# Key norms of an RWKV-7 mixer from compact tiles with tokens on the partitions, and gate and merge matmuls dealt in half steps to the recurrence's chunks

## Chip, cores and metric

One core of one Trainium2 chip. The metric is the device time of one execution in microseconds (us): the median of three runs.

## What is computed

The reference is a two-layer encoder trunk on 512 tokens of width 1024, in float32. Each layer has a mixer with three branches (pooling, differential attention, a bidirectional RWKV-7 recurrence), merged by sigmoid gates, then an output projection, a layer norm, a squared-ReLU MLP and another layer norm. The parts that the change touches:

```python
kk = kh * heads(k_k)                                   # 8 heads of 64
kk = kk / max(sqrt(sum(kk * kk, -1, keepdims=True)), 1e-12)
y  = wkv7_scan(..., kk, a, forward) + wkv7_scan(..., kk, a, reverse)
...
branch = einsum('bsnc,ncd->bsnd', [y_a, y_b, y_c], w_branch)
gates  = sigmoid(gl + b_gate)                          # 3 x 1024 columns of x @ w_in
mixer  = sum(gates * branch, over the 3 branches) @ w_out
```

## The kernel before

Activations lie transposed: channels on the 128 partitions, the 512 tokens on the free axis. Almost every product of a dense weight is taken three times in a 32-bit replicated form (`mm3`: high x high, high x low, low x high), so each weight tile is split into a high part (a ScalarE cast, L142) and a low part (a subtraction, L143, mostly on GpSimd). A dense tile of 128 output channels is 8 x 3 = 24 matmuls of 512 columns.

A layer runs in stages, in `layer`:

1. `rw_prep` makes the recurrence's factors, channel tile by channel tile (j = 0 to 3); `weave` deals pooling and attention matmuls between its steps. A generator yields the microseconds of TensorE work that it has emitted, and `weave` hands out filler until its sum is `ratio` times the main generator's sum.
2. `rw_solve`, first part: a triangular solve, thirty dependent pairs of VectorE operations (L650, L652). The filler is `gates(0)` and `merge(0)`; what is left of it is drained.
3. `rw_solve`, second part: small matmuls (32 or 64 rows and columns) that build the matrix `tt`. Six steps of `merge(1)` are emitted first, and the rest is dealt at ratio 0.8. These filler steps are emitted by `behind`: on TensorE they may not go ahead of the last small matmul before them.
4. `rw_chain`: eight chunks of 64 tokens, c = 0 to 7, each with steps that depend on each other: `pb x suv`, the products of the next chunk's rows, `x tt`, `qk` and `rq`, and two groups of transposed copies. Here TensorE's order is the order in which the code emits (a manual schedule); on the other engines and on the DMA queues the planner of the framework chooses the order from a simulated timeline. Each chunk loads the next one's products `ch` by DMA; `ch` has two buffers, and its load can begin only when the last group of transposes of the chunk has read the old one.
5. The end of the chain: from chunk 6 the filler is `rw_out(0)` (group norm and gate of the middle tokens) and what is left of the gates. Then `rw_out(1)` (the outer tokens) with the first four steps of `merge_last`, and the rest of `merge_last`, the projection and the MLP.

For the key norms, `rw_prep` squares a key tile, `head_sums` sums the squares per head with two 512-column matmuls against a block of ones (L528, L529), which leaves each head's sum on all its 64 partitions, and `rsqrt` takes the inverse root of the 128 x 512 tile by a bit shift and three Newton steps on VectorE (L211 to L218).

Of the kernel before, what the change touches and what calls it, by code (L numbers as in the profile page):

```python
# [18 lines left out]
S = 512  # L19
# [30 lines left out]
FILL = (1.7, 25.0, 2.0, 1.2, 1.2, 6, 0.8)  # L50
# [71 lines left out]
class Enc:  # L122
# [81 lines left out]

    def rsqrt(self, pool, x, shape, tags, bufs=1, out=None):

        V = self.nc.vector
        t = self.T(pool, shape, tags[0], bufs)
        g = t.bitcast(I32)
        y = self.T(pool, shape, tags[1], bufs, I32)  # L210
        V.tensor_scalar(g, x.bitcast(I32), 1, None, ALU.logical_shift_right)  # L211
        V.tensor_scalar(y, g, -1.0, float(0x5F3759DF), ALU.mult, ALU.add)
        yf = y.bitcast(F32)
        out = yf if out is None else out
        for i in range(3):
            V.tensor_tensor(t, yf, yf, ALU.mult)
            V.scalar_tensor_tensor(t, t, -0.5, x, ALU.mult, ALU.mult)
            V.scalar_tensor_tensor(out if i == 2 else yf, t, 1.5, yf, ALU.add, ALU.mult)  # L218
        return out
# [160 lines left out]
    def layer(self, l):  # L380
# [6 lines left out]
        with tc.tile_pool(name=f"R{l}", bufs=1) as self.R:  # L387
            rt = ExitStack()
            with ExitStack() as at:
                self.AT = at.enter_context(tc.tile_pool(name=f"AT{l}", bufs=1, side="right"))  # L390
                self.RX = at.enter_context(tc.tile_pool(name=f"X{l}", bufs=1, side="right"))
                att = chain(self.pool_branch(), self.attention())
                with tc.tile_pool(name=f"A{l}", bufs=1) as self.R1:
                    weave(self.rw_prep(), att, FILL[0], FILL[1])
                    drain(att)
                self.RT = rt.enter_context(tc.tile_pool(name=f"T{l}", bufs=1))
                with tc.tile_pool(name=f"B{l}", bufs=1) as self.R2:
                    fill = chain(self.gates(0), self.pool_load(), self.merge(0))
                    steps = self.rw_solve()
                    weave(self.urgent(steps), fill, FILL[2])  # L400
                    drain(fill)
                    fill = chain(self.merge(1), self.gates(2))
                    for _ in range(int(FILL[5])):
                        next(fill)
                    fill = self.behind(fill)
                    weave(self.urgent(steps), fill, FILL[6])
            with rt, tc.tile_pool(name=f"C{l}", bufs=1) as self.R3:
                steps = self.rw_chain()
                with tc.manual_schedule(engines={mybir.EngineType.PE}):
                    weave(self.urgent(steps), fill, FILL[3])  # L410
                    fill = alternate(self.rw_out(0), fill)
                    weave(self.urgent(steps), fill, FILL[4])
                    drain(fill)
                last = self.merge_last()
                weave(self.urgent(self.rw_out(1)), self.behind(islice(last, 4)), 1.0)
# [53 lines left out]
    def rw_prep(self):  # L469
# [5 lines left out]
        pss = self.lora_ps  # L475
        if l == 0:
# [15 lines left out]
        for j in range(4):  # L492
# [3 lines left out]
            ps = self.head_sums(sq)  # L496
            rs = self.T(R1, [128, S], "sq", 1)
            V.tensor_scalar(rs, ps, 1e-24, None, ALU.max)
            rs = self.rsqrt(R1, rs, [128, S], ("ld", "ta"))
            kk = self.T(R1, [128, S], "kk", 1)  # L500
            V.scalar_tensor_tensor(kk, k, self.pcol(P_KK + j), rs, ALU.mult, ALU.mult)
# [17 lines left out]
            yield 0.4  # L519

# [580 lines left out]
    def gate(self, n, m, gw, dst):  # L1101
# [3 lines left out]
        for k in range(NK):  # L1105
            self.mm3(ps, wh[:, k, :], wl[:, k, :], self.xh[:, k, :], self.xl[:, k, :], k == 0, k == NK - 1)
            if k % 4 == 3:
                yield 2.6
# [21 lines left out]
    def merge(self, n):  # L1130
# [5 lines left out]
        for m in range(NK):  # L1136
# [8 lines left out]
            for k in range(4):  # L1145
                self.mm3(ps, wh[:, k], wl[:, k], *y[k], k == 0, k == 3)
            V.scalar_tensor_tensor(g, g, 1.0, ps, ALU.add, ALU.mult)
            if n:
                nc.gpsimd.tensor_tensor(self.mg[m], self.mg[m], g, ALU.add)
            yield 2.6  # L1150
# [190 lines left out]
```

## Time and profile before

| | |
|---|---|
| median of three runs | 2178.73 us (2174.46 to 2180.32) |
| the profiled execution | 2177.25 us, span 2175.4 us |
| TensorE (PE) busy | 2070.0 us, 95% of the span |
| VectorE (DVE) busy | 1109.1 us, 51% |
| ScalarE (ACT) busy | 858.7 us, 39% |
| GpSimd (POOL) busy | 611.5 us, 28% |
| mean granted TensorE clock | 0.961 of full speed |

Matmuls overlap each other in the pipeline, so a busy TensorE is not one at its peak; a matmul's row gives its length from start to end, and the distance between the starts of neighbours is what it costs. The clock has two levels, 1.2 GHz (0.50) and 2.4 GHz (1.00); a figure between them is a mean over a stretch. 2177.25 us is the profiled execution's own time, 1.85 us more than its span.

### The profile page before, as it was taken

The numbers are of one execution on the slowest core, as the hardware profiler recorded it, in microseconds if no ns is written. First come the engines' busy times: TensorE is split into PE (matmuls) and PEld (weight loads), VectorE is DVE, ScalarE is ACT, GpSimd is POOL, SyncE is SP. The second block draws the span as 40 slices with busy tenths as digits, with TensorE's granted clock in tenths as the row PEclk, the third lists the DMA queues.
The fourth block names the chain that finished last, engine by engine and source line by source line (L and its number), as shares of the span: only waits on it lengthen the run. The fifth ranks groups of instructions, "written<-read, shape, count | busy, mean of one in ns | idle before, by whom it ended". The sixth has DMA issues, their size and how long they took to land.

```text
span 2175.4 us, 32525 instructions
## 1 busy us (share of the span) xinstructions
PE 2070.0 (95%) x13382; PEld 1647.2 (76%) x13382; DVE 1109.1 (51%) x1760; ACT 858.7 (39%) x1341; POOL 611.5 (28%) x407
## 2 busy tenths in 40 slices
PE   6999999999979999999998999999998899999998
PEld 5667776777767888888886776778777688888886
DVE  5878769322246443343266878782222445423423
ACT  5355555324323332232344555562333243322322
POOL 4543353133215400000445433431322163000004
PEclk9999999889979999999999999997999799999999
DMA  6343341145523332332424334411545052323322
GB/s 209 115 131 105 121 156 59 40 110 148 137 72 119 98 93 97 97 97 97 140 93 131 120 97 128 134 59 38 151 130 148 21 176 67 97 97 97 90 95 87
DMA packets 309680, 233.63 MB, mean 107 GB/s; under 512 B 50106, under 2 KB 277880, under 8 KB 309532
## 3 DMA queue, kind: packets, MB, share of 16 engines
q1 hardware_dynamic: 309388, 231.30, 35.6%
q8 instruction: 105, 1.72, 0.3%
q10 hardware_dynamic: 144, 0.26, 0.1%
q14 instruction: 43, 0.35, 0.1%
HBM read 200.05 MB, written 31.47 MB: 106 GB/s over the span
## 4 chain that ended last, share of the span: by engine, by line
PE 67%; DVE 14%; DMA 7%; POOL 4%; ACT 4%; issue 3%; SPq 0%; POOLq 0%; DVEq 0%; ACTq 0%
PE d L166 13%; PE d L168 12%; PE d L167 12%; PE a L162 5%; PE c L162 3%; DMA ch<-sc 3%; PE l L166 2%; PE l L167 2%; PE l L168 2%; DVE x L652 2%; PE t L162 2%; DVE at L650 1%; PE a L166 1%; PE a L167 1%; PE a L168 1%
## 5 line engine op out<-in xcount | busy, mean ns | idle before, releaser
L166 PE MATMUL d<-xh,wh 128*128 128x512 f32 (+1 forms) x1360 | 546.8, 402 | 6.7 <-ACT xh L268 2.4
L168 PE MATMUL d<-xh,wl 128*128 128x512 f32 (+1 forms) x1360 | 538.8, 396 | 0.8 <-POOL wl L143 0.7
L167 PE MATMUL d<-xl,wh 128*128 128x512 f32 (+1 forms) x1360 | 537.4, 395 | 0.0
L143 POOL TENSOR_TENSOR wl<-wraw,wh 128x1024 fp32r<-128x1024 f32 x137 | 337.9, 2468 | 530.1 <-ACT wh L142 507.1
L142 ACT CAST wh<-wraw 128x1024 fp32r<-128x1024 f32 x259 | 271.3, 1048 | 517.8 <-PE d L167 208.0
L143 DVE TENSOR_TENSOR wl<-wraw,wh 128x1024 fp32r<-128x1024 f32 x122 | 160.6, 1317 | 368.2 <-ACT wh L142 368.1
L166 PEld LDWEIGHTS d<-xh,wh 128*128 128x128 f32 x1360 | 258.9, 191 | 78.9 <-issue 14.1
L168 PEld LDWEIGHTS d<-xh,wl 128*128 128x128 f32 x1360 | 258.8, 190 | 67.0 <-issue 7.1
L167 PEld LDWEIGHTS d<-xl,wh 128*128 128x128 f32 x1360 | 259.3, 191 | 57.6 <-issue 3.1
L143 POOL TENSOR_TENSOR wrl<-wraw,wrh 128x1024 fp32r<-128x1024 f32 x16 | 39.2, 2465 | 659.6 <-ACT wrh L142 659.6
L1266 ACT CAST hh<-f 128x512 fp32r<-128x512 f32 x64 | 39.7, 622 | 84.5 <-DVE f L1263 84.5
L1267 DVE TENSOR_TENSOR hl<-f,hh 128x512 fp32r<-128x512 f32 x64 | 44.2, 693 | 41.4 <-ACT hh L1266 41.3
L795 DVE COPY x<-c 128x256 f32<-128x256 f32 x16 | 6.8, 424 | 112.7 <-ACT x L794 112.7
L977 ACT ACTIVATE p<-p,mx 128x512 f32<-128x512 f32 x64 | 46.0, 719 | 43.6 <-DVE mx L976 43.3
L162 PE MATMUL a<-ch 64*128 64x128 f32 x512 | 53.0, 311 | 10.6 <-DMA ch<-sc 10.6
L162 PEld LDWEIGHTS a<-ch 64*128 64x128 f32 x512 | 42.5, 206 | 15.1 <-issue 7.0
L652 DVE TENSOR_TENSOR x<-x,at 128x60 f32<-128x60 f32 (+14 forms) x60 | 51.1, 851 | 1.5
L1263 DVE TENSOR_TENSOR f<-f 128x512 f32<-128x512 f32 x64 | 43.6, 684 | 14.8 <-ACT f L1262 14.8
L758 DVE TENSOR_TENSOR rq<-a,cst 128x256 f32<-128x256 f32 x64 | 27.2, 425 | 44.1 <-PE a L162 31.6
L975 DVE CUSTOM_DVE_ANT_0 p<-l,tb 128x512 f32<-128x512 f32 x64 | 42.5, 683 | 13.8 <-PE t L990 9.6
L168 PE MATMUL l<-wh,hl 128*128 128x512 f32 x112 | 43.6, 389 | 0.0
L167 PE MATMUL d<-wl,hh 128*128 128x512 f32 x112 | 43.6, 389 | 0.0
(531 smaller groups left out, 4039.3 us busy)
## 6 DMA issues: line engine op xcount, KB each, us to landing
wraw<-in_w_in_dram SPq DMA_DIRECT2D x110, 512.0 KB
wraw<-in_w_up_dram SPq DMA_DIRECT2D x64, 512.0 KB
wraw<-in_w_down_dram SPq DMA_DIRECT2D x64, 512.0 KB
sc<-st SPq DMA_DIRECT2D x16, 1280.0 KB
ch<-sc SPq DMA_DIRECT2D x32, 640.0 KB
wraw<-in_w_branch_dram SPq DMA_DIRECT2D x24, 512.0 KB
wraw<-in_w_out_dram SPq DMA_DIRECT2D x16, 512.0 KB
xs<-s SPq DMA_DIRECT2D x16, 256.0 KB
```

Source lines behind the costliest of these rows:

```text
L142: self.nc.scalar.copy(hi, src)
L143: (eng or self.nc.vector).tensor_tensor(lo, src, hi, ALU.subtract)
L162: self.anchor = self.nc.tensor.matmul(*args, **kw).ins
L166: mm(out, wh, xh, start=first, stop=False)
L167: mm(out, wh, xl, start=False, stop=False)
L168: mm(out, wl, xh, start=False, stop=last)
L652: V.tensor_tensor(ab[:, s + 1:, :, :s], ab[:, s + 1:, :, :s], w, ALU.add)
L975: V.tensor_tensor_reduce(p, ps, bias, op0=ALU.add, op1=ALU.max, scale=1.0, scalar=-3e38, accum_out=mx)
L977: A.activation(p, p, AF.Exp, bias=mx, accum_out=sm[:, m:m + 1])
L1263: V.tensor_tensor(f, f, f, ALU.mult)
L1266: A.copy(hi, f)
L1267: V.tensor_tensor(lo, f, hi, ALU.subtract)
```

## The change

It has two parts. First, the key norms: the sums per head are taken with the tokens on the partitions (four matmuls with the squares as the stationary operand and two columns of ones moving), which gives a 128 x 8 tile; VectorE clamps it, GpSimd raises it to the power -0.5, TensorE transposes it, ScalarE and VectorE split it into a high and a low part, and eight 128-column selector matmuls spread it over the heads' partitions in PSUM, where `kk`'s multiplication reads it. `rsqrt` goes.

Second, the filler: `gate` and `merge` yield after 6 matmuls (1.3) instead of 12 (2.6); the six steps ahead of the second part of the solve go; the chain's ratio is 0.7 instead of 1.2 up to chunk 5 and 1.4 instead of 1.2 after it; the end deals `rw_out(0)` and then `rw_out(1)` in turn with whatever filler is left, all in the manual order.

```diff
-FILL = (1.7, 25.0, 2.0, 1.2, 1.2, 6, 0.8)
+FILL = (1.7, 25.0, 2.0, 0.7, 1.4, 0.8)
...
                     fill = chain(self.merge(1), self.gates(2))
-                    for _ in range(int(FILL[5])):
-                        next(fill)
                     fill = self.behind(fill)
-                    weave(self.urgent(steps), fill, FILL[6])
+                    weave(self.urgent(steps), fill, FILL[5])
             with rt, tc.tile_pool(name=f"C{l}", bufs=1) as self.R3:
                 steps = self.rw_chain()
                 with tc.manual_schedule(engines={mybir.EngineType.PE}):
                     weave(self.urgent(steps), fill, FILL[3])
-                    fill = alternate(self.rw_out(0), fill)
-                    weave(self.urgent(steps), fill, FILL[4])
-                    drain(fill)
-                last = self.merge_last()
-                weave(self.urgent(self.rw_out(1)), self.behind(islice(last, 4)), 1.0)
+                    last = self.merge_last()
+                    both = alternate(self.rw_out(0), chain(fill, islice(last, 4)))
+                    weave(self.urgent(steps), both, FILL[4])
+                    drain(self.urgent(alternate(self.rw_out(1), both)))
...
-            ps = self.head_sums(sq)
-            rs = self.T(R1, [128, S], "sq", 1)
-            V.tensor_scalar(rs, ps, 1e-24, None, ALU.max)
-            rs = self.rsqrt(R1, rs, [128, S], ("ld", "ta"))
             kk = self.T(R1, [128, S], "kk", 1)
-            V.scalar_tensor_tensor(kk, k, self.pcol(P_KK + j), rs, ALU.mult, ALU.mult)
+            V.scalar_tensor_tensor(kk, k, self.pcol(P_KK + j), self.norms(sq), ALU.mult, ALU.mult)
...
+    def norms(self, sq):
+        nc, R1, V = self.nc, self.R1, self.nc.vector
+        ps = self.acc("c")[:, :8].rearrange("p (t q) -> p t q", t=4)
+        for t in range(4):
+            nc.tensor.matmul(ps[:, t, :], sq[:, t * 128:(t + 1) * 128], self.cst[:, C_BLK:C_BLK + 2], start=True, stop=True)
+        ve = self.T(R1, [128, 4, 2], "ve", 2)
+        V.tensor_scalar(ve, ps, 1e-24, None, ALU.max)
+        nc.gpsimd.tensor_tensor(self.nrs[:, :, :2], ve, self.mhalf.unsqueeze(2).to_broadcast([128, 4, 2]), ALU.pow)
+        ps = self.acc("c")[:, :128]
+        nc.tensor.transpose(ps, self.nrs.rearrange("p t q -> p (t q)"), self.ident)
+        rows = self.T(R1, [128, S], "sq", 1, F32R)
+        hi, lo = rows[:, :128], rows[:, 128:256]
+        nc.scalar.copy(hi, ps)
+        V.tensor_tensor(lo, ps, hi, ALU.subtract)
+        ps = self.acc("a")
+        for t in range(4):
+            for i, x in enumerate((hi, lo)):
+                nc.tensor.matmul(ps[:, t * 128:(t + 1) * 128], self.sel[:, 128 * t:128 * t + 128], x, start=i == 0, stop=i == 1)
+        return ps
...
-            if k % 4 == 3:
-                yield 2.6
+            if k % 2 == 1:
+                yield 1.3
...
             for k in range(4):
                 self.mm3(ps, wh[:, k], wl[:, k], *y[k], k == 0, k == 3)
+                if k == 1:
+                    yield 1.3
             V.scalar_tensor_tensor(g, g, 1.0, ps, ALU.add, ALU.mult)
             if n:
                 nc.gpsimd.tensor_tensor(self.mg[m], self.mg[m], g, ALU.add)
-            yield 2.6
+            yield 1.3
```

## Rows read from the trace of the kernel before

**Rows 1.** The profile's page: its span, the busy time of each engine (share of the span, instructions), and the granted TensorE clock in 40 equal slices (tenths of full speed, 9 for 90% or more).

```profile
span 2175.4 us, 32525 instructions
...
PE 2070.0 (95%) x13382; PEld 1647.2 (76%) x13382; DVE 1109.1 (51%) x1760; ACT 858.7 (39%) x1341; POOL 611.5 (28%) x407
...
PEclk9999999889979999999999999997999799999999
```

**Rows 2.** Busy time of each engine by stretch: the stretch and its length, busy us (and instructions) of PE, weight loads, DVE, ACT and POOL, granted clock, DMA share, GB/s. Layer 0: prep 50 to 320, first part of the solve to 386, second part to 455, chunks 0 to 5 to 603, the end of the chain to 676. Layer 1: prep 1120 to 1395, second part of the solve 1475 to 1525, chunks to 1673, end to 1746.

```profile
50.00:320.00 270.00, 262.07 (x1282) 190.68 (x1282) 216.85 (x365) 146.00 (x254) 117.57 (x71) 0.99 0.40 123
320.00:380.00 60.00, 55.96 (x255) 41.84 (x254) 52.38 (x89) 34.44 (x57) 23.07 (x11) 0.94 0.23 71
380.00:386.00 6.00, 4.66 (x27) 2.88 (x26) 5.76 (x12) 3.83 (x6) 2.98 (x3) 1.00 0.54 157
386.00:404.00 18.00, 18.00 (x162) 14.70 (x160) 7.76 (x10) 9.66 (x13) 2.37 (x1) 1.00 0.13 37
404.00:455.00 51.00, 51.00 (x608) 42.18 (x606) 11.65 (x18) 9.63 (x14) 11.74 (x10) 0.70 0.12 32
455.00:603.00 148.00, 142.23 (x1662) 115.10 (x1661) 40.04 (x81) 49.82 (x81) 44.42 (x33) 1.00 0.55 143
603.00:676.00 73.00, 55.18 (x634) 47.67 (x634) 32.54 (x66) 19.40 (x35) 12.35 (x7) 0.81 0.20 58
1120.00:1395.00 275.00, 266.73 (x1305) 195.10 (x1304) 208.47 (x356) 149.67 (x259) 117.72 (x71) 0.98 0.40 121
...
1475.00:1525.00 50.00, 50.00 (x612) 41.68 (x611) 11.62 (x18) 9.63 (x14) 11.45 (x9) 0.73 0.12 32
1525.00:1673.00 148.00, 143.38 (x1678) 115.87 (x1678) 40.09 (x82) 50.35 (x82) 44.71 (x33) 1.00 0.55 144
1673.00:1746.00 73.00, 57.22 (x614) 49.90 (x611) 31.22 (x64) 18.24 (x35) 12.30 (x7) 0.74 0.20 57
```

**Rows 3.** Who TensorE waited for in the end of the chain of layer 0 (603 to 676): waiting line, releaser, us in total, times, longest.

```profile
PE a L162 <- ACT qk L774: 6.0, 3, 3.2
PE d L166 <- ACT yah L918: 2.3, 1, 2.3
PE l L898 <- DVE f L900: 1.9, 2, 1.0
PE a L162 <- DMA ch<-sc: 1.5, 1, 1.5
```

**Rows 4.** TensorE in order of time around one chunk of layer 0, and its last filler matmul: start, us, line, operation, count, in brackets the idle time before and its releaser.

```profile
539.28 0.50 PE L166 MATMUL d<-xh,wh 128*128 128x512 f32 x1
...
542.27 1.15 PE L162 MATMUL c<-suv,pb 128*64 128x64 f32 x32
544.00 1.34 PE L162 MATMUL a<-ch 64*128 64x128 f32 x16 [0.57 <-DMA ch<-sc]
545.26 0.50 PE L166 MATMUL d<-xh,wh 128*128 128x512 f32 x1
...
548.26 1.15 PE L162 MATMUL c<-x,tt 64*64 64x64 f32 x32
...
557.15 1.15 PE L162 MATMUL c<-suv,qk 128*64 128x64 f32 x32
...
559.81 0.50 PE L166 MATMUL d<-xh,wh 128*128 128x512 f32 x1
...
562.80 0.71 PE L162 MATMUL a<-cst,ch 64*128 64x64 f32 x16
...
603.05 0.40 PE L168 MATMUL d<-xh,wl 128*128 128x512 f32 x1
```

**Rows 5.** The same chunk on ScalarE and on the DMA queue of SyncE; then TensorE at chunk 0.

```profile
561.11 1.08 ACT L774 COPY qk<-a 128x512 f32<-128x512 f32 x2
539.13 0.52 SPq L701 DMA_DIRECT2D ch<-sc  x1
474.53 1.56 PE L162 MATMUL a<-ch 64*128 64x128 f32 x16 [1.73 <-DMA ch<-sc]
```

**Rows 6.** Two waits of TensorE and the granted clock around them: the wait at 331 (timeline), the two stretches around it, and the stretch that holds the wait of chunk 0 (columns as in rows 2).

```profile
331.08 0.40 PE L639 MATMUL a<-cst,x 128*64 128x128 f32 x1 [2.07 <-ACT tt L644]
330.00:335.00 5.00, 3.80 (x6) 1.78 (x7) 4.70 (x13) 4.11 (x8) 2.43 (x2) 0.55 0.32 105
335.00:340.00 5.00, 5.00 (x19) 3.86 (x18) 3.24 (x8) 0.96 (x3) 0.00 (x0) 0.76 0.00 0
470.00:475.00 5.00, 3.27 (x44) 2.43 (x42) 0.42 (x1) 1.89 (x3) 2.31 (x1) 1.00 0.94 282
```

**Rows 7.** Operations like those that the change removes and adds, by line (first 800 us; count, busy us, mean ns; one row with the least, median and greatest ns instead), and three stretches of TensorE (start, us, line, count).

```profile
L217 DVE SCALAR_TENSOR_TENSOR ld<-ld,sq 128x512 f32<-128x512 f32 x12 | 14.5, 1206 | 0.2
L217 DVE SCALAR_TENSOR_TENSOR ld<-ld,sq x12: 670/692/2768, 71.0 to 267.4; 128x512 f32<-128x512 f32 x12
L216 DVE TENSOR_TENSOR ld<-ta 128x512 f32<-128x512 f32 x12 | 12.4, 1032 | 0.2
L218 DVE SCALAR_TENSOR_TENSOR ta<-ld,ta 128x512 f32<-128x512 f32 x12 | 10.5, 871 | 0.2
L211 DVE TENSOR_SCALAR ld<-sq 128x512 int32<-128x512 int32 x4 | 4.2, 1057 | 0.1
L1011 POOL TENSOR_TENSOR ve<-ve,mhalf 128x8 f32<-128x8 f32 x4 | 6.9, 1718 | 9.0 <-DVE ve L1010 9.0
327.14 0.95 PE L1009 MATMUL t<-cst,f 128*128 128x2 f32 x8
327.95 0.60 PE L639 MATMUL a<-cst,x 128*64 128x128 f32 x4
638.17 0.74 PE L913 MATMUL l<-rw,sel 128*128 128x256 f32 x4
```

**Rows 8.** The longest waits of TensorE in the prep of layer 0 (50 to 320) and of layer 1 (1115 to 1395).

```profile
PE l L1083 <- DVE f L1081: 1.5, 3, 0.8
PE l L1083 <- DVE f L1081: 4.6, 1, 4.6
```

More of the change, by code (lines that the diff above doesn't have):

```diff
@@ L203, in dense @@
         return ps
[L205 to L219, printed above, removed]
     def ln_params(self, L, g, b):
@@ L475, in rw_prep @@
         pss = self.lora_ps
+        self.nrs = self.T(R1, [128, 4, 32], "rs", 1)
+        G.memset(self.nrs, 0.0)
         if l == 0:
```

## The prediction

> **What bounds the kernel now.** The page comes first. TensorE is busy 95% of the span and the next engine 51% [rows 1], so only three things can move the end: work taken from or put on TensorE, its idle time (105 us in all), and the time in which its clock stands at 1.2 GHz. The slices of the clock show where that is: two dips per layer. So the second view is the table by stretch [rows 2]. In it, prep is full (262 of 270 us, clock 0.99). The solve's second part is full but slow (clock 0.70 and 0.73). Chunks 0 to 5 lose only 5.8 and 4.6 us of 148 and keep the clock. The end of the chain loses most: 73 - 55.2 = 17.8 us idle and about 0.19 x 55.2 = 10.5 us through the clock in layer 0, 15.8 and 0.26 x 57.2 = 14.9 us in layer 1. The third view is the list of waits there [rows 3]: ScalarE's copies of `qk`, the group norm's VectorE steps, a DMA. These are latencies of the chain and of `rw_out`, which nothing covers, because the last filler matmul starts at 603.05 [rows 4]: 15.6 + 13 + 1.2 x 67.6 nominal us were dealt up to the end of chunk 5, and there are only 104.
>
> **The deal after the change.** Counting `weave` through by hand in half steps (6 matmuls, 1.3 nominal): 9 go to the solve's second part, 37 to chunks 0 to 5, 12 between chunks 6 and 7, and 22 to the end, 5 of them between the steps of `rw_out(1)` and 17 behind it. Matmuls of 512 columns start 0.233 us apart (12 and a change of shape in 545.26 to 548.26, 3.0 us [rows 4]), so a half step costs 1.4 us, 1.6 with the change of shape. No filler is saved; about 34 x 1.4 = 48 us of it per layer move from the solve and the chunks to the end.
>
> *The end.* Its chain latencies now lie under filler. What stays idle: the load of `ch` in chunk 6 with one half step before it (2.1, worked out below), the group norm's `g2` products, which go through `l` banks that VectorE must empty and which took 1.9 [rows 3] and now also wait for `bv`, whose `f2` buffer the last `merge(1)` step holds (3 in all), a bank shared with that step (0.5), and about 2 in `rw_out(1)`: 7.6 us for 17.8 and 15.8. For the clock I keep 2.5 us of loss for 10.5 and 14.9. Together -18.2 and -20.6 us.
>
> *The chunks.* Here the cover becomes thin, at two places. First `ch`: the last transposes end at 539.28, the load is issued at 539.13 and lands at 544.00 (rows 4 and 5 show the three times [rows 4, 5]), 4.7 us after those transposes. TensorE was 0.57 us too early with a full step (3.0) between. With one half step (1.6) it is 1.4 earlier: 2.1 us. The deal puts two half steps there before chunks 1 and 4, one before chunks 2, 3, 5 and 6. Before chunk 0 there was a full step and still 1.73 [rows 5]; now there is none: 4.7. Sum for chunks 0 to 5: 4.7 + 2 x 0.7 + 3 x 2.1 = 12.4. Second `qk`: the third step starts at 557.15, its matmuls end at 559.81, ScalarE ends the copies at 562.19 [rows 4, 5]. With one half step TensorE is there at 561.4, 0.8 early; this happens in four of six chunks, and I put 0.2 on the other two: 3.6. Idle in the chunks is then 16 for 5.8 and 4.6: +10.2 and +11.4. Bounds: nothing, if the planner finds the load an earlier place (no reason in the code: the buffer is read until then), and 1.3 more per chunk where a GpSimd split stretches VectorE's additions. For the clock: 4.7 us of nothing will drop it once, about 3 us. Chunks +13.2 and +14.4.
>
> *The solve.* Without the six steps, the bare end of the first part (1.34 idle of 6 us, VectorE busy 5.76 of them [rows 2]) has some 12 matmuls fewer, up to 2.8 us, and 386 to 404 has some 24 fewer. Against this, VectorE is the engine that sets the end of the first part, and the other edit frees it. Bounds: -5.4, if all idle time from 320 to 386 goes; +3 idle and 9 us of small matmuls at half the rate, +12, and 10 more if 404 to 455 falls from 0.70 to 0.50. I take +3 per layer, nearest to the idle row.
>
> *The norms.* On VectorE each key tile loses nine Newton operations, the two bit operations, one clamp and one subtraction: 14.5 + 12.4 + 10.5 + 4.2 [rows 7], and about 7 more for the rest, some 49 us of 217 in prep [rows 2]. TensorE loses two matmuls (0.47 us) per tile. It gets four sums (eight records from 327.14 to 327.95 [rows 7], 0.8), a transpose (0.15), and eight 128-column selectors, between half of and as much as the 256-column one, whose starts lie 0.12 apart (0.48 to 0.96; 0.72): +1.2 per tile, +4.8 per layer. GpSimd's power took 1.7 us [rows 7] and can stand behind a weight split; TensorE's transpose waits for it in order, and behind it stands the next dense tile; who waits for that is all of prep. Bounds: 0, if a projection lies between (5.6 us), and 2.4 per tile; I take 0.5 per tile, 2 per layer. What can be won is prep's idle time and dips: 7.9 + 2.7 and 8.3 + 5.5 us [rows 2], mostly waits on VectorE, one of them 4.6 us long [rows 8]. VectorE loses a fifth of its load and the pairs that GpSimd stretches (1206 ns mean where the median is 692 [rows 7]); I take two thirds: -7.1 and -9.2. Norms -0.3 and -2.4.
>
> **Sum.** Layer 0: -18.2 + 13.2 + 3 - 0.3 = -2.3; layer 1: -20.6 + 14.4 + 3 - 2.4 = -5.6. Together -7.9 us, from 2177.25 for the profiled execution (1.5 below the median of the runs) to 2169. What looks like a gain of 39 us at the end is for the most part paid back in the chunks.
>
> **Rivals.** *The chunks lose the clock* (slower). The new waits of 2.1 us stand between small matmuls. After one of 2.07 us at 331 the clock fell to 1.2 GHz, 0.55 and 0.76 over the next ten us: 3.8 x 0.45 + 5 x 0.24 = 2.9 us lost [rows 6]. Against it: around chunk 0's wait of 1.73 it stayed at 1.00 [rows 6]. Eight such waits (chunks 2, 3, 5, 6) cost 8 x 2.9 = 23: 2192. Three of them bring the change back to nothing, six make it slower than measurement can hide. The Trainium skill, page "TensorE: Matmul & The Clock Gate", section "HAM oscillation — how this bites in real kernels", tells of just this: a DMA wait in every turn of a loop throttles the clock again in every turn. By that rule the rival would be the likelier case; the trace agrees at 331 and not at chunk 0, so it keeps a smaller chance here.
>
> *The solve stands bare* (slower): the 24 and 12 matmuls are not replaced and the small ones run at half rate from 386 on: 9 more per layer, 2187. For it: clock 0.70 already in the next stretch; against it: TensorE has no idle time at all there [rows 2].
>
> *The exchange is even*: the chunks and the solve take all that the end and prep give, 2178. The planner's new order of the other engines, which no row shows, can do that alone.
>
> **Chances.** A run can tell 0.3%, 6.5 us. The forecast (2150 to 2172) 0.45, even 0.27, clock in the chunks 0.17, bare solve 0.11. So faster 0.45, the same 0.27, slower 0.28. The range takes in the two slower rivals, to 2194, and below it the case in which the end loses nothing more and the chunks no clock (-25 + 10 for one layer, -28 + 11 for the other, solve and prep as in the sum less 2 each: 2147): 2149 to 2194. The forecast's own range is 2158 to 2172.
>
> **What would show it.** Right: the end of the chain at clock 0.95 or more with under 9 us idle; waits for `ch` of about 2 us in four places per layer and one near 5 at chunk 0; VectorE's total 100 us lower; prep with no wait over 2 us. Wrong: clock below 0.95 between chunks 0 and 5, a solve that is longer with less filler in it, TensorE's transposes waiting for GpSimd's power for more than 0.5 us per tile, or a `bv` that comes so late that `rw_out(0)` holds the whole queue.

## The result: 1.3% slower

The changed kernel took 2205.95 us (median of four runs, 2201.99 to 2208.75); the kernel before, on the same chip, 2178.42. The ratio is 1.0127, 95% interval 1.0106 to 1.0149: 27.5 us slower, where 2169 was forecast, and 12 us above the range. The profiled execution took 2207.05 us.

The page of the profile after (span, busy time of the engines, clock in 40 slices; before in [rows 1]):

```profile
span 2205.3 us, 32700 instructions
PE 2086.4 (95%) x13502; PEld 1659.0 (75%) x13502; DVE 1007.4 (46%) x1672; ACT 860.6 (39%) x1341; POOL 618.5 (28%) x417
PEclk9999999589999999999999999986999999999999
```

VectorE lost 102 us, as forecast (100), and the kernel got slower. Of the clock's two dips per layer, the one at the end of the chain is gone and the one in the solve is deeper. So the layers are cut at landmarks instead of at fixed times: the last transposes of `at` (prep ends), the first 64x32 products (the solve's first part ends), the first `suv x pb` (the second part ends), the first group norm product of the outer tokens, and the last product of `merge_last`. By these cuts, the kernel before (columns as in [rows 2]; prep, solve 1, solve 2, chain, end of layer 0, then the same of layer 1):

```profile
50.00:325.20 275.20, 267.27 (x1308) 194.65 (x1307) 219.42 (x367) 148.41 (x257) 120.42 (x72) 0.99 0.40 124
325.20:385.60 60.40, 55.02 (x250) 40.38 (x248) 55.17 (x96) 35.86 (x58) 23.21 (x12) 0.94 0.22 66
385.60:471.60 86.00, 85.11 (x870) 69.31 (x869) 22.11 (x34) 24.24 (x35) 21.37 (x16) 0.82 0.22 61
471.60:653.10 181.50, 162.42 (x2051) 132.54 (x2050) 58.84 (x118) 58.32 (x99) 42.73 (x31) 0.92 0.45 119
653.10:686.20 33.10, 29.48 (x185) 26.38 (x186) 21.62 (x32) 13.47 (x20) 16.72 (x8) 1.00 0.41 143
1100.00:1398.10 298.10, 289.83 (x1481) 217.45 (x1481) 220.70 (x374) 159.84 (x275) 121.64 (x78) 0.98 0.39 119
1398.10:1457.60 59.50, 53.99 (x251) 39.98 (x249) 55.20 (x96) 35.93 (x59) 24.02 (x12) 0.97 0.22 67
1457.60:1541.70 84.10, 83.21 (x870) 68.31 (x869) 22.08 (x34) 24.27 (x35) 21.41 (x16) 0.84 0.22 62
1541.70:1723.70 182.00, 165.33 (x2051) 135.32 (x2051) 58.95 (x118) 58.29 (x99) 42.70 (x31) 0.91 0.45 118
1723.70:1757.80 34.10, 31.26 (x186) 27.98 (x187) 21.44 (x33) 13.76 (x21) 15.21 (x8) 0.95 0.39 139
```

And the changed kernel by the same landmarks (layer 0 ends 10 us later here, so the prep of layer 1 is counted from 1110 for 1100):

```profile
50.00:332.20 282.20, 276.67 (x1400) 205.54 (x1400) 172.89 (x334) 154.31 (x267) 128.56 (x78) 0.99 0.40 123
332.20:393.00 60.80, 47.62 (x212) 34.00 (x211) 56.48 (x94) 32.65 (x53) 17.91 (x9) 0.91 0.20 61
393.00:464.10 71.10, 67.38 (x778) 55.05 (x778) 14.23 (x22) 16.90 (x25) 8.68 (x9) 0.67 0.14 35
464.10:632.90 168.80, 153.10 (x2014) 123.58 (x2015) 58.71 (x120) 53.53 (x93) 41.06 (x33) 0.95 0.46 121
632.90:696.10 63.20, 60.67 (x318) 50.77 (x317) 21.58 (x34) 23.64 (x33) 29.53 (x14) 1.00 0.43 142
1110.00:1417.60 307.60, 301.11 (x1577) 228.91 (x1577) 184.14 (x346) 166.51 (x286) 133.40 (x86) 0.99 0.38 118
1417.60:1478.00 60.40, 47.73 (x213) 34.04 (x213) 56.39 (x94) 32.61 (x52) 17.87 (x9) 0.91 0.20 61
1478.00:1551.50 73.50, 70.51 (x777) 58.02 (x777) 14.24 (x22) 16.91 (x25) 8.58 (x9) 0.63 0.13 33
1551.50:1725.00 173.50, 155.73 (x2015) 125.33 (x2016) 58.69 (x120) 53.62 (x93) 41.12 (x33) 0.94 0.45 118
1725.00:1789.60 64.60, 62.08 (x319) 51.95 (x318) 21.62 (x34) 23.75 (x33) 29.59 (x14) 0.97 0.43 138
```

A stage's length says little here, since filler was moved between stages. What is lost in one is its idle time (length less PE busy) and what its clock takes (PE busy times one less the clock). In us, layer 0 and layer 1:

| | before | after | difference | forecast |
|---|---|---|---|---|
| prep | 7.9 + 2.7; 8.3 + 5.8 | 5.5 + 2.8; 6.5 + 3.0 | -2.3; -4.6 | -7.1; -9.2 |
| solve 1 | 5.4 + 3.3; 5.5 + 1.6 | 13.2 + 4.3; 12.7 + 4.3 | +8.8; +9.9 | solve 1 and 2: |
| solve 2 | 0.9 + 15.3; 0.9 + 13.3 | 3.7 + 22.2; 3.0 + 26.1 | +9.7; +14.9 | +3; +3 |
| chain and its end | 22.7 + 13.0; 19.5 + 16.5 | 18.2 + 7.7; 20.3 + 11.2 | -9.8; -4.5 | -5.0; -6.2 |

The exchange between the chunks and the end came out near its sum. Prep won less than forecast. The solve missed by most: +18.5 and +24.8 us for +3 and +3. Its first part is no longer and no shorter (60.8 for 60.4 us, VectorE busy 56.48 for 55.17): its VectorE chain sets it, and it has less filler in it. TensorE there, by line (dense products of the gates and the idle time in front of the solve's transposes), before and then after:

```profile
L168 PE MATMUL d<-xh,wl 128*128 128x512 f32 x23 | 9.9, 430 | 0.0
L167 PE MATMUL d<-xl,wh 128*128 128x512 f32 x23 | 9.7, 422 | 0.0
L166 PE MATMUL d<-xh,wh 128*128 128x512 f32 x22 | 9.7, 440 | 0.0
L639 PE MATMUL a<-cst,x 128*64 128x128 f32 x31 | 8.2, 279 | 4.4 <-DVE x L652 2.1 <-ACT tt L644 2.1
```
```profile
L640 PE MATMUL a<-cst,x 128*64 128x128 f32 x31 | 9.1, 303 | 7.9 <-DVE x L653 7.8
L167 PE MATMUL d<-xl,wh 128*128 128x512 f32 x13 | 5.4, 414 | 0.0
L168 PE MATMUL d<-xh,wl 128*128 128x512 f32 x13 | 5.3, 409 | 0.0
L166 PE MATMUL d<-xh,wh 128*128 128x512 f32 x12 | 4.8, 402 | 0.0
```

Thirty gate products fewer (68 to 38). Twelve of them belonged to the six steps (e4 below, the kernel before without them, has 56). The other 18 were done before prep's end: prep holds 262 products of each of the three gate and projection forms before and 268 after. The end of the first part then looks like this (the stretch from the last filler of `gates` and `merge` to the solve's second part, and the next 11 us):

```profile
377.90:393.00 15.10, 6.12 (x15) 2.56 (x15) 13.37 (x25) 7.16 (x13) 2.54 (x1) 0.63 0.12 35
393.00:404.00 11.00, 9.99 (x80) 8.44 (x81) 1.04 (x1) 5.21 (x7) 0.00 (x0) 0.50 0.01 1
```

9.0 us idle of 15.1, then the small products at 1.2 GHz throughout, where the kernel before had them at clock 1.00 from 386 to 404 [rows 2].

The chain needs a closer look, because the mean clock of the whole of it (0.92 and 0.91 before, 0.95 and 0.94 after) hides two things that go opposite ways. At the end, from chunk 6 on, the clock's loss fell. In chunks 0 to 5, where the kernel before stood at 1.00 [rows 2], the changed kernel's clock now falls. Its chunks 0 to 5 in layer 0 and in layer 1, then two waits for `ch` in layer 0 and the clock just behind each:

```profile
464.10:585.00 120.90, 109.95 (x1536) 88.81 (x1536) 38.99 (x81) 38.25 (x67) 27.16 (x25) 0.96 0.52 134
1551.50:1677.00 125.50, 112.27 (x1534) 90.38 (x1536) 38.99 (x81) 38.34 (x67) 27.23 (x25) 0.95 0.51 130
```
```profile
467.68 2.34 PE L162 MATMUL a<-ch 64*128 64x128 f32 x16 [1.88 <-DMA ch<-sc]
529.18 1.33 PE L162 MATMUL a<-ch 64*128 64x128 f32 x16 [1.34 <-DMA ch<-sc]
469.00:474.00 5.00, 5.00 (x19) 3.91 (x17) 1.60 (x4) 0.00 (x0) 0.00 (x0) 0.50 0.92 178
529.00:534.00 5.00, 4.82 (x86) 4.16 (x86) 2.40 (x6) 0.58 (x1) 1.02 (x1) 1.00 1.02 252
```

Of the seven loads for `ch` in each layer, the clock fell to 0.50 after three in layer 0 (waits of 1.88, 2.44 and 1.83 us) and after four in layer 1 (2.34, 2.48, 2.20 and 1.63), and stayed at 1.00 after the other seven (0.5 to 1.62 us). The length of the wait alone does not decide it: behind the 1.73 us of the kernel before it stayed at 1.00 [rows 6]. Read in stretches of 1 us, these falls cost 1.7 to 3.3 us each, 15 us in all.

### The profile page after: what moved, and what is told of

It reads as the page before. It is cut to its first block, busy times and chain, and to the rows that moved or that the text cites. A ratio compares the mean times of both kernels' runs of the same rounds, so it can differ in the third digit from the quotient of the medians.

```text
span 2205.3 us, 32700 instructions
## 1 busy us (share of the span) xinstructions
PE 2086.4 (95%) x13502; PEld 1659.0 (75%) x13502; DVE 1007.4 (46%) x1672; ACT 860.6 (39%) x1341; POOL 618.5 (28%) x417
## 4 chain that ended last, share of the span: by engine, by line
PE 76%; DVE 8%; DMA 6%; POOL 4%; ACT 3%; issue 2%; SPq 0%; POOLq 0%; DVEq 0%; ACTq 0%
PE d L166 15%; PE d L168 15%; PE d L167 15%; PE a L162 5%; DMA ch<-sc 3%; PE c L162 3%; PE l L166 2%; PE l L167 2%; PE l L168 2%; PE t L162 2%; DVE x L653 2%; PE a L166 1%; PE a L167 1%; PE a L168 1%; PE l L973 1%
## 5 line engine op out<-in xcount | busy, mean ns | idle before, releaser
L143 POOL TENSOR_TENSOR wl<-wraw,wh 128x1024 fp32r<-128x1024 f32 x137 | 333.2, 2434 | 480.7 <-ACT wh L142 452.4
L162 PE MATMUL a<-ch 64*128 64x128 f32 x512 | 47.1, 308 | 21.9 <-DMA ch<-sc 21.9
L978 ACT ACTIVATE p<-p,mx 128x512 f32<-128x512 f32 x64 | 46.0, 719 | 22.7 <-DVE mx L977 22.7
L645 ACT COPY tt<-a 32x256 f32<-32x256 f32 x64 | 38.5, 602 | 22.3 <-PE a L640 21.7
```

The source lines that it names most:

```text
L143: (eng or self.nc.vector).tensor_tensor(lo, src, hi, ALU.subtract)
L162: self.anchor = self.nc.tensor.matmul(*args, **kw).ins
L978: A.activation(p, p, AF.Exp, bias=mx, accum_out=sm[:, m:m + 1])
```

## The experiments

The ratio in each is to the kernel before, with its 95% interval; losses are read as above, layer 0 and layer 1. The expectations of e1 to e4 weigh two theories, S (the solve's missing filler) and N (the norms).

**e1: the new norms, the old deal.**

```diff
-            ps = self.head_sums(sq)
...
-            V.scalar_tensor_tensor(kk, k, self.pcol(P_KK + j), rs, ALU.mult, ALU.mult)
+            V.scalar_tensor_tensor(kk, k, self.pcol(P_KK + j), self.norms(sq), ALU.mult, ALU.mult)
```

> The kernel before with the new key norms alone; the deal of the filler, the six steps ahead of the solve's second part included, is the old one. The change as a whole costs 27.5 us. Theory S (the loss is the solve, whose filler the deal took away): the norms alone give TensorE some 5 us more work per layer and take 2 to 3 us of prep's waits away, so 0 to +10 us, and the first part of the solve has under 8 us of idle TensorE per layer because the six steps still lie there. Theory N (the norms themselves cost: freed VectorE lets attention run earlier, prep ends later, and the solve has less left to cover it): +12 to +25 us, prep ends 5 us or more later in each layer.

Measured 2178.21 us, 1.0005 (0.9989 to 1.0022). Alone the norms cost and bring nothing. Idle time of the solve's first part 6.5 and 6.2 us: with the six steps there it stays covered. In the second part, though, the clock is 0.76 and 0.80 for 0.82 and 0.84.

**e2: the new deal, the old norms.**

```diff
-FILL = (1.7, 25.0, 2.0, 1.2, 1.2, 6, 0.8)
+FILL = (1.7, 25.0, 2.0, 0.7, 1.4, 0.8)
...
-            if k % 4 == 3:
-                yield 2.6
+            if k % 2 == 1:
+                yield 1.3
```

> The kernel before with the new deal alone (half steps, no six steps, ratios 0.7 and 1.4, both rw_out in turn with the filler); the key norms are the old ones. Theory S: most of the loss, +12 to +27 us; TensorE's clock in the solve's second part under 0.75 in both layers. Theory N: within 8 us of the kernel before, as the gain at the end of the chain and the cost in the chunks and the solve cancel.

Measured 2192.52 us, 1.0076 (1.0057 to 1.0096). Some 0.8 of the 1.3% is the deal's; the rest comes only when both parts are there, since e1 has nothing. First part idle 7.6 and 7.7 us, second part at clock 0.65 and 0.64.

**e3: the six steps back, as twelve half steps.**

```diff
                     fill = chain(self.merge(1), self.gates(2))
+                    for _ in range(12):
+                        next(fill)
                     fill = self.behind(fill)
```

> The changed kernel with the filler ahead of the solve's second part put back (12 half steps, the same 72 matmuls as the old six steps); norms and everything else of the deal stay new. Theory S: the idle time of the solve's first part falls from 13 to under 8 us per layer and the clock of its second part rises from 0.65 to 0.80 or more; at least 15 us of the 27.5 come back, so at most +12 us against the kernel before. Theory N: less than 8 us come back, +20 us or more.

Measured 2179.27 us, 1.0021 (1.0006 to 1.0037): 23 us of the 27.5 are back. Idle 6.7 and 6.3 us in the first part, clock there 1.00 and 0.98. The clock of the second part rose only to 0.74 and 0.73, where S had 0.80 or more.

**e4: the kernel before without its six steps.**

```diff
-FILL = (1.7, 25.0, 2.0, 1.2, 1.2, 6, 0.8)
+FILL = (1.7, 25.0, 2.0, 1.2, 1.2, 0, 0.8)
```

> The kernel before with only the six filler steps ahead of the solve's second part left out; they then go to the chunks and the end of the chain in the old full steps. Theory S: the solve loses 8 to 14 us per layer, of which 5 to 8 come back at the end of the chain, whose filler now lasts about a chunk longer: +4 to +16 us. Theory N: no change beyond 5 us, since VectorE's load in prep is the old one.

Measured 2158.45 us, 0.9924 (0.9903 to 0.9944). Both theories missed: S had it slower, N level. With the old norms, taking the six steps out gains 0.8%, some 16 us: they cover the chain and its end instead (idle 13.3 and 12.3, clock loss 8.8 and 5.2 in the chain, 19.1, 16.7, 13.0 and 14.9 before), and the solve's first part is only 2 us barer (7.4 and 7.6 idle). With its clock (0.75 and 0.72 in the second part) the solve loses 4.9 and 9.2 us more than before, less than the chain and its end win.

**e5: the change with full steps, in `gate` and in `merge`.**

```diff
-            if k % 2 == 1:
-                yield 1.3
+            if k % 4 == 3:
+                yield 2.6
```

> The changed kernel with the old full steps of 12 matmuls in gate and merge; ratios, order and norms stay new. Theory H (a half step of 6 matmuls is too short a dense stretch to lift the clock in the solve's second part): its clock goes from 0.67 and 0.63 to 0.72 or more, the stretch loses 5 to 8 us less per layer, and the whole is 10 to 18 us faster than the changed kernel, +10 to +18 us against the kernel before. Rival (the size of a step does not matter, only how many matmuls the solve gets): within 6 us of the changed kernel, +22 us or more.

Measured 2219.54 us, 1.0205 (1.0187 to 1.0223). Slower by 14 us than the change, which neither case had: half steps are not what costs the time. Why full steps cost more here was not followed up.

**e6: e1 without the six steps.**

```diff
-FILL = (1.7, 25.0, 2.0, 1.2, 1.2, 6, 0.8)
+FILL = (1.7, 25.0, 2.0, 1.2, 1.2, 0, 0.8)
```

> The kernel before with the new norms and without the six steps; steps and ratios old. Without the six steps alone the kernel was 18.7 us faster than before. Theory X (the new norms take away what the first part of the solve lives on once the six steps are gone): idle time of the solve's first part 12 us or more per layer, against 7.5, and the whole between -12 and -4 us. Rival (the two edits add up): -16 to -20 us, since the norms alone measured +1 us.

Measured 2190.76 us, 1.0072 (1.0056 to 1.0088). Here is the interaction: with the six steps the new norms change nothing (e1), without them they cost 1.5% (e6 against e4). First part idle 13.4 and 13.2 us, as expected, second part at 0.64 and 0.69. The time was not: 15 us slower than the kernel before, where 4 to 12 us faster was expected.

**e7: the kernel before with the new end, ratios 1.0 and 1.4, no six steps.**

```diff
-FILL = (1.7, 25.0, 2.0, 1.2, 1.2, 6, 0.8)
+FILL = (1.7, 25.0, 2.0, 1.0, 1.4, 0.8)
...
-                    fill = alternate(self.rw_out(0), fill)
...
+                    both = alternate(self.rw_out(0), chain(fill, islice(last, 4)))
+                    weave(self.urgent(steps), both, FILL[4])
+                    drain(self.urgent(alternate(self.rw_out(1), both)))
```

> The old norms, old full steps, no six steps, chain ratio 1.0 up to chunk 5 instead of 1.2, and the new end (rw_out(0) and rw_out(1) in turn with the filler that is left, ratio 1.4). If the new end is worth what the sum gave it and thin chunks cost the rest, the chunks keep a full step before nearly every load, the last chunks get filler, and this is 3 to 12 us faster than the kernel without the six steps: -20 to -30 us against the kernel before. If the loss comes from the new end, it is slower than that kernel: above -15 us.

Measured 2162.58 us, 0.9942 (0.9927 to 0.9958). By the expectation's own line (above -15 us) this falls on the side of a new end that costs. But it is 4 us from e4, within the noise, and the share for the chunks differs too (1.0 for 1.2), so the run shows only that the new end brings nothing over e4, not that it harms.

**e8: more filler dealt to the solve's second part.**

```diff
-FILL = (1.7, 25.0, 2.0, 0.7, 1.4, 0.8)
+FILL = (1.7, 25.0, 2.0, 0.7, 1.4, 2.0)
```

> The changed kernel with ratio 2.0 instead of 0.8 in the solve's second part: 22 half steps there instead of 9, 13 fewer at the end. Theory S (the loss is filler missing from the solve's second part): its clock rises from 0.65 to 0.80 or more, 8 us less lost per layer, +8 to +16 us against the kernel before. Rival (the loss lies in the first part of the solve and in prep, which this leaves alone): within 6 us of the changed kernel, +22 us or more.

Measured 2225.27 us, 1.0225 (1.0206 to 1.0243), the slowest of all. Neither case had it this slow. `behind` keeps this filler out of the first part, which is as bare as in the change (idle 13.2). The second part (96.7 us) now has 150 matmuls of 512 columns for 72 and still runs at clock 0.70 in both layers, and the chain then lacks it (18.2 and 20.1 idle).

**e9: the attention dealt to prep at 1.4.** What has to be told apart now: is the time lost because work has left the solve (A), or in prep itself, through the norms' hop over GpSimd and ScalarE (P)?

```diff
-FILL = (1.7, 25.0, 2.0, 0.7, 1.4, 0.8)
+FILL = (1.4, 25.0, 2.0, 0.7, 1.4, 0.8)
```

> The changed kernel with the attention dealt to prep at 1.4 in place of 1.7 (first number of FILL), nothing else. Theory A (the freed VectorE lets 18 of the first gates' matmuls and more of the attention run ahead of prep's end; what the solve's first part then lacks is idle time and clock): between prep's last transposes and the end of the solve's first part more 512-column matmuls stand than the changed kernel's 154; idle time there falls from 13.2 and 12.7 us to about 6, the clock of the solve's second part rises above 0.70, and of the 27 us lost some 12 to 20 come back: 2186 to 2194. Rival P (the norms' hop over GpSimd, TensorE and ScalarE in prep costs the time, by idle TensorE in prep): less filler in prep makes that worse, 2206 to 2220.

Measured 2181.43 us, 1.0017 (1.0000 to 1.0033): 24 us back, by a little more than A gave. Prep, solve 1, solve 2 and chain of layer 0:

```profile
50.00:314.70 264.70, 261.46 (x1339) 193.61 (x1338) 174.39 (x323) 146.31 (x254) 119.42 (x74) 1.00 0.41 125
314.70:375.60 60.90, 54.81 (x242) 40.88 (x240) 54.87 (x95) 35.11 (x58) 20.96 (x11) 0.92 0.23 70
375.60:451.90 76.30, 73.75 (x811) 60.19 (x811) 21.80 (x33) 21.65 (x33) 14.65 (x13) 0.75 0.14 36
451.90:627.50 175.60, 156.88 (x2014) 125.93 (x2015) 58.81 (x120) 53.67 (x93) 41.08 (x33) 0.92 0.46 120
```

Prep is 17.5 us shorter with 3.2 us of idle time; the first part's length is the same to 0.1 us and 7 us of its idle time are filled; the second part runs at 0.75. e3 and e9 cover the same bare stretch by different means; the two together were not run.

**e10: the first gates held behind prep's end.**

```diff
-                nc.tensor.transpose(ps[:, i * 128:(i + 1) * 128], at[:, :, :, tl].rearrange("p b q -> p (b q)"), self.ident)
+                self.anchor = nc.tensor.transpose(ps[:, i * 128:(i + 1) * 128], at[:, :, :, tl].rearrange("p b q -> p (b q)"), self.ident).ins
...
-                    fill = chain(self.gates(0), self.pool_load(), self.merge(0))
+                    fill = chain(self.behind(self.gates(0)), self.pool_load(), self.merge(0))
```

> The changed kernel with the first gates held behind prep's last transposes; the attention is dealt as in the changed kernel. Theory A: the solve's first part is full (idle under 5 us per layer, clock 0.95 or more), prep ends 15 to 25 us earlier but has more idle time, since the gates filled it; the sum decides how much: 2178 to 2196. If the bare solve is not the cause, idle time moves from the solve into prep and nothing comes back: 2203 to 2215.

Measured 2215.03 us, 1.0177 (1.0162 to 1.0193): the case of idle time that moves, and 9 us more than the change. Prep and solve 1 of layer 0:

```profile
50.00:324.40 274.40, 262.96 (x1301) 192.81 (x1300) 170.43 (x343) 147.16 (x261) 112.40 (x71) 0.94 0.37 115
324.40:378.70 54.30, 49.49 (x224) 37.83 (x222) 50.30 (x71) 34.03 (x51) 25.95 (x12) 0.94 0.26 79
```

The first part is full (4.8 us idle) as A said, but prep, without the gates that covered it, has 11.4 us idle and loses 15.8 by its clock. Both stages need cover, and the gates can be in only one of them. A as I had put it, a loss in the solve alone, is too simple: which filler goes where matters.

**e11: the old VectorE work left on, with no use.**

```diff
+        ld = self.T(R1, [128, S], "ld", 1)
+        ta = self.T(R1, [128, S], "ta", 1)
+        V.tensor_scalar(ld, sq, 0.0, None, ALU.mult)
+        for i in range(3):
+            V.tensor_tensor(ta, ld, ld, ALU.mult)
+            V.scalar_tensor_tensor(ta, ta, -0.5, sq, ALU.mult, ALU.mult)
+            V.scalar_tensor_tensor(ld, ta, 1.5, ld, ALU.add, ALU.mult)
         ve = self.T(R1, [128, 4, 2], "ve", 2)
```

One scaling and nine operations of the loop make ten per key tile; the expectation's seven is a miscount.

> The changed kernel with seven VectorE operations over 128x512 per key tile put back in front of the clamp, on scratch tiles; their result goes nowhere. It does more work than the changed kernel. Theory A (it is the relief of VectorE that lets work run ahead of prep's end): idle time in the solve's first part falls from 13 to about 9 us and the time stays the same or falls, 2195 to 2206. Rival P (the chain of the norms itself is the cost): the longer chain adds its 4 to 5 us per tile or a good part of it, 2212 to 2235.

Measured 2196.64 us, 1.0099 (1.0075 to 1.0123): 9 us faster than the change, with more work in it. The trace is of the slowest of its four executions (2205.02 us), so it shows where the work went and not the 9 us. Prep and solve 1 of layer 0:

```profile
50.00:330.90 280.90, 273.32 (x1383) 203.67 (x1382) 203.87 (x364) 152.07 (x259) 128.50 (x77) 0.99 0.40 122
330.90:390.90 60.00, 51.02 (x227) 37.27 (x226) 52.46 (x99) 35.61 (x59) 20.14 (x10) 0.93 0.23 69
```

VectorE is 31 us busier in prep and the solve has 15 more matmuls in its first part (227 for 212), 9.0 us of idle time for 13.2. So a VectorE that is slower in prep does hold work back for the solve. P said 2212 or more and falls.

**e12: e6 with the attention at 1.4.**

```diff
-FILL = (1.7, 25.0, 2.0, 1.2, 1.2, 0, 0.8)
+FILL = (1.4, 25.0, 2.0, 1.2, 1.2, 0, 0.8)
```

> The new norms with the old deal less its six steps (2190.8 in an earlier run, against 2158.5 with the old norms), the attention at 1.4 in place of 1.7. Theory A: the 31 us between those two come back for the most part: 2160 to 2172, idle time of the solve's first part 6 to 8 us in place of 13. Rival P: 2188 to 2200.

Measured 2153.19 us, 0.9890 (0.9872 to 0.9908): more than the 31 us come back, and it beats both kernels. Against e4 it is 0.3% faster, at the edge of the noise: the two intervals just overlap.

**e13: e9 with the chunks' share back at 1.2.**

```diff
-FILL = (1.4, 25.0, 2.0, 0.7, 1.4, 0.8)
+FILL = (1.4, 25.0, 2.0, 1.2, 1.4, 0.8)
```

> The kernel of e9 (2181.4) with the chunks' share of filler back at 1.2 from 0.7; half steps and the new end stay. If the share is what leaves the chain bare, its idle time falls from 18.7 and 18.2 us to about 12 and its clock loss from 12.6 and 9.3 to under 7, and the time to 2155 to 2165, near e12. If the half steps themselves are the cost (too small a piece at a time ahead of each wait), 2172 to 2185.

Measured 2153.46 us, 0.9898 (0.9878 to 0.9919): the whole change with two numbers of `FILL` set otherwise, level with e12, which has neither half steps nor the new end: these bring nothing here. Solve 1, solve 2 and chain of layer 0:

```profile
315.10:377.00 61.90, 54.92 (x242) 41.05 (x240) 56.03 (x95) 35.99 (x60) 22.14 (x11) 0.92 0.22 69
377.00:453.30 76.30, 74.68 (x825) 60.47 (x824) 21.85 (x33) 22.15 (x33) 17.63 (x15) 0.78 0.16 44
453.30:641.80 188.50, 178.80 (x2183) 146.68 (x2183) 58.48 (x120) 62.87 (x104) 52.73 (x36) 0.99 0.48 129
```

The chain is idle for 9.7 us (18.7 in e9) and loses 1.8 by its clock (12.6). The share was what left it bare, not the half steps. The filler that the chain gets is missing at the end, whose clock is 0.79 in both layers, a loss of 6 us each.

**e14: e4 with the attention at 1.4.**

```diff
-FILL = (1.7, 25.0, 2.0, 1.2, 1.2, 0, 0.8)
+FILL = (1.4, 25.0, 2.0, 1.2, 1.2, 0, 0.8)
```

> The old norms, the old deal without its six steps, and the attention at 1.4: e4 (2158.5) with the thinner attention, or e12 (2153.2) with the old norms. If the thinner attention is what helped in e12 and the new norms are worth nothing, 2148 to 2156. If VectorE's relief in prep is worth what it was forecast at (some 8 us per layer of idle time and dips), prep here is idle for longer than e12's 3.3 and 2.3 us, and the time is 2160 to 2172.

Measured 2165.65 us, 0.9948 (0.9933 to 0.9963). With the old norms the thinner attention does harm (e4 has 0.9924), with the new ones it is a gain. The prep of layer 1 from 1100 us on, here (in the slowest of ten executions, 2173.91 us) and then in e12:

```profile
1100.00:1380.10 280.10, 269.80 (x1382) 203.43 (x1381) 211.23 (x344) 147.04 (x250) 110.29 (x74) 0.96 0.39 118
```
```profile
1100.00:1373.10 273.10, 270.78 (x1425) 203.62 (x1425) 173.28 (x322) 152.68 (x264) 116.66 (x76) 1.00 0.40 121
```

10.3 us idle and 10.8 by the clock with the old norms, 2.3 and nothing with the new ones; the longest wait there is again that of [rows 8], 4.6 us. At 1.4 the norms are worth 12 us (e14 to e12). But 1.4 is the wrong ratio for the old norms; each kind at the better of its two ratios, e12 against e4, they are worth 5 to 7 us, near what a run can tell.

**e15: the share alone.**

```diff
-FILL = (1.7, 25.0, 2.0, 0.7, 1.4, 0.8)
+FILL = (1.7, 25.0, 2.0, 1.2, 1.4, 0.8)
```

> The changed kernel with the chunks' share of filler at 1.2 in place of 0.7 and nothing else; e13 less the thinner attention. If the two causes are separate and add up, the share alone gives back its 28 us: 2174 to 2182, with the solve's first part as bare as in the changed kernel (idle about 13 us). If the bare solve eats what the share gives, as in e6, 2186 to 2196.

Measured 2180.22 us, 1.0016 (1.0003 to 1.0029). Solve 1 and chain of layer 0:

```profile
332.20:393.00 60.80, 47.61 (x213) 34.01 (x212) 56.31 (x94) 32.66 (x52) 17.86 (x9) 0.91 0.20 60
466.00:653.30 187.30, 180.50 (x2184) 147.91 (x2184) 58.54 (x120) 62.97 (x104) 52.72 (x37) 0.98 0.48 128
```

The first part is as bare as in the change, the chain is covered (6.8 us idle). With e9 and e13 this closes a square of the attention's ratio and the chunks' share, in ratios to the kernel before:

| | share 0.7 | share 1.2 |
|---|---|---|
| attention 1.7 | 1.0127 (the change) | 1.0016 (e15) |
| attention 1.4 | 1.0017 (e9) | 0.9898 (e13) |

Each costs about 1.1%, 24 to 26 us, with or without the other. They are two separate losses. What is left without them, 1.0% faster than the kernel before (e13), is little more than the 0.8% of e4.

## Why the prediction was wrong

**The step that failed is the solve's, "I take +3 per layer".** Measured: +18.5 and +24.8. Three things in it were wrong.

*The cover.* It set against the missing filler that "VectorE is the engine that sets the end of the first part, and the other edit frees it". The first half is right and the second is not. The norms are work of prep; in the first part VectorE is as busy as before, 56.5 us of 60.8. What the relief did was to let prep's TensorE work go on sooner, and the planner drew 18 gate products and the end of the attention from the solve ahead of prep's end. e11 shows the direction: load VectorE in prep again, and 15 matmuls and 4 us of cover return to the solve.

*The count.* It took 12 and 24 filler matmuls out of the two parts. By lines, products of 512 columns fell from 180 to 154 and from 165 to 72: 119 fewer. The six steps are 72 of them. 18 more are the gates that went ahead, and some five the attention's or at the edges of the stretches. The last 24 are the difference between the eight full steps (96) of e6's second part and the twelve half steps (72) here. By the deal, five of the eight and nine of the twelve are the solve's own at ratio 0.8, 6 matmuls fewer by rounding; the other three of each are the first of the chain's share, now in half steps, 18 fewer. The counts of e8 (22 and 3 half steps, 150) and e15 (9 and 5, 84) agree with this.

*The price.* The bounds were right to list it: small products at half rate and idle time, up to +22. Layer 0 came out inside, layer 1 above. I chose the value next to the idle row (TensorE with no idle time from 386 on) when the clock's row beside it, 0.70 from 404 on, was the one that bore on a stretch of small products with less filler in it.

**The rival of the bare solve** had the right place and the right sign, at 0.11, and 12 us per layer (the sum's 3 and 9 more) where 22 came. Its mechanism was half of the truth; that the norms' edit would make it worse was in no case of mine.

**The end and the chunks** were right, as a sum (-9.8 and -4.5 for -5.0 and -6.2) and apart. Read in stretches of 1 us, chunks 0 to 5 lost 11 and 16 us more (for +13.2 and +14.4), the end from chunk 6 on 18 and 20 us less (for -18.2 and -20.6). The waits of the chain (layer 0):

```profile
PE a L162 <- DMA ch<-sc: 9.9, 7, 2.4
PE l L899 <- DVE f L901: 2.4, 2, 1.3
PE a L162 <- ACT qk L775: 2.0, 8, 0.3
```

`ch` 9.9 us (12.0 in layer 1) in seven waits (nine) for the 14.5 of the sum with chunk 6; the long one at chunk 0 did not come (the longest is 2.4). `qk` 2.0 for 3.6, `g2` 2.4 for 3. From chunk 6 on, 7.3 and 7.0 us are idle for the 7.6 of the sum. So the exchange is a fair reading of the kernel before. But it took for a gain of the whole deal what the removal of the six steps gives by itself (e4: -0.8%), and the smaller share for the chunks was not needed: that alone costs 1.1% (e15, e13).

**The rival of the clock in the chunks** came in good part, at 0.17. It had eight waits of about 2 us at 2.9 us each, 23 us; the clock fell after seven, for 15 us. The sum had 3 us per layer for it, where chunks 0 to 5 alone lost 4.8 and 6.8 us. It did not decide the result: with it, the chunks and the end still came out near their forecasts. The Trainium skill, page "TensorE: Matmul & The Clock Gate", section "HAM oscillation — how this bites in real kernels", tells of a clock that falls in every turn of a loop that waits for a DMA in each; this trace agrees in seven turns of fourteen.

**The norms.** TensorE never waited for GpSimd's power (no such row among prep's waits; 0.5 per tile was taken). The power took 1.65 us each (1.7 in [rows 7]). But the gain in prep was put too high: -2.3 and -4.6 us came for -7.1 and -9.2, and waits of 2.5 and 3.6 us for `kk` stood where none over 2 was forecast. Idle time in layer 0 fell from 7.9 to 5.5 us, not by two thirds, because the attention crowded in; with the attention at 1.4 it falls to 3.2 (e9), near what was forecast. So "norms -0.3 and -2.4" is not far from e1 (1.0005), but for a reason that the sum did not have: prep of layer 0 won 2.4 us there, and the solves of the two layers lost 2.3 and 3.6 us more.

**What stays open:** the cut between idle and clock losses is only as fine as the clock's two digits, about 2 us in prep and more in the MLP. The rows of the table add up to 22 us where the spans differ by 29.9; the TensorE work that the norms add, 9.6 us for both layers by the sum, is no loss and stands in no row. And which wait of VectorE in prep decided that the planner drew the gates ahead was not followed up.

## What to carry to other kernels

- An engine that is made faster in one stage lets the filler of the next stage run ahead. Count, in the stage behind it, which filler is left, before the relief is booked as a gain; here the ratio that deals the filler had to be cut from 1.7 to 1.4 with it, and with that cut the new norms came out ahead of the old ones (by 12 us at 1.4, by 5 to 7 when each has its better ratio).
- A stage whose length is set by another engine's chain is worth just the filler that lies under it: what is taken out is idle time there and slow clock behind it.
- When several ratios are changed together, each can be a separate loss; a square of four runs told them apart and found a version 1.0% faster than the kernel before and 2.3% faster than the change. Run the simplest edit by itself, too: leaving out the six steps alone gave 0.8 of that 1.0% (e4).
- A mean over a stage can hide its parts: the chain's clock rose on the whole while it fell in chunks 0 to 5.

## What the runs showed of the hardware

The granted clock of the solve's second part differed much between kernels, though TensorE was busy for 95 to 99% of it in each and the small products are the same: 0.67 and 0.63 in the change (72 filler matmuls among them, after a first part with 13 us idle), 0.75 and 0.72 in e4 (104, after 7.5 us idle), 0.82 and 0.84 before (165, after 5.4). Idle time there is small in all three; what is lost is the clock, 22 to 26 us per layer in the change. That filler taken from a stretch costs more than its own time in that stretch had not been expected. Both the filler inside and the stretch ahead count, by three more runs. e8 has 150 after the change's bare first part, and 0.70 in both layers: filler inside does not make up for it. e6 has 96, close to e4's 104, but after 13 us idle, and 0.64 and 0.69. e2 has 80 after the 7.6 us idle of e4, and 0.65 and 0.64. How much each weighs was not told apart.

One operation of the solve's chain was stretched nearly fivefold. VectorE in order of time near the end of the first part, after:

```profile
377.79 0.54 DVE L651 TENSOR_TENSOR at<-x 128x368 f32<-128x368 f32 x1
378.36 2.57 DVE L653 TENSOR_TENSOR x<-x,at 128x368 f32<-128x368 f32 x1
```

The addition over 368 elements took 2.57 us, its neighbour of the same shape 0.54; TensorE's longest wait in the solve's first part, 2.81 us, is for this addition. GpSimd had a weight split under way just then:

```profile
377.99 2.54 POOL L143 TENSOR_TENSOR wl<-wraw,wh 128x1024 fp32r<-128x1024 f32 x1 [5.26 <-ACT wh L142]
```

It ends at 380.53, and the addition 0.4 us later, at 380.93. The Trainium skill, page "SBUF — State Buffer", section "SBUF: two separate sides", tells of such a pair: VectorE and GpSimd share a pair of ports, which one of them holds for its whole operation while the other is blocked. The trace agrees: the addition, with both inputs in SBUF, got through when the split was done. It is not the change's doing: the kernel before has two such additions, of 2.73 and 2.66 us, each ending 0.3 to 0.5 us after a split. One thing does not fit: the multiplication at 377.79 overlaps the split's first 0.34 us and is not stretched.
